# 512 KB weight loads with four pairs of split tiles, and modulation sums in halves, in a hybrid mLSTM and gated-delta encoder block

## The chip, the cores and the metric

The kernel runs on 1 core of a Trainium2 chip. The metric is the device time of one execution in microseconds, the median over runs. TensorE (PE) does the matmuls, with its weight loads shown apart as PEld; VectorE (DVE), ScalarE (ACT) and GpSimd (POOL) do the rest; SyncE (SP) issues most of the DMAs, which 16 DMA engines carry out.

## The reference

One encoder block with batch 1, 256 tokens and width 2048, all in float32. Its weights are some 480 MB and each is used once, so they stream from HBM for the whole run.

```python
c_act = jax.nn.silu(c)
mod = c_act @ ada_w + ada_b                       # 2048 x 12288
shift_m, scale_m, gate_m, shift_f, scale_f, gate_f = jnp.split(mod[:, None, :], 6, axis=-1)
h = rms_norm(x, norm_mix_w) * (1 + scale_m) + shift_m
proj = h @ w_in                                   # split into a_q, a_k, a_v, a_o, a_i, a_f, b_qkv, b_z, b_beta, b_a, merge
h_a = bidirectional(mlstm_chunkwise, ...)         # 4 heads, dk 256, dv 512
y_a = (sigmoid(a_o) * rms_norm(h_a)) @ w_branch_a
o_b = bidirectional(gated_delta_chunkwise, ...)   # 16 heads of 128, chunks of 64, a triangular solve in each
y_b = (rms_norm(o_b) * silu(b_z)) @ w_branch_b
g_a, g_b = jnp.split(jax.nn.sigmoid(merge), 2, axis=-1)
x = x + gate_m * ((g_a * y_a + g_b * y_b) @ w_out)
hf = rms_norm(x, norm_ffn_w) * (1 + scale_f) + shift_f
gt, up = jnp.split(hf @ w_gate_up, 2, axis=-1)
x = x + gate_f * ((silu(gt) * up) @ w_down)       # d_ff 5632
return rms_norm(x, norm_final_w)
```

`mod`, the modulation, is what the change calls by that name: a vector times a 2048 x 12288 matrix, of which two sixths are needed at once and four sixths later.

## The kernel before

**Precision in three products.** A float32 weight is split on the chip: `wh` is its value rounded to the fp32r type (ACT, a copy), `wl` is the remainder (DVE, a subtraction). The activations are split in the same way into a high and a low part, such as `hh`, `hl` for the input projection and `mgh`, `mgl` for `o`. Each product is three matmuls: high by `wh`, low by `wh`, high by `wl`.

**Jobs.** Nearly all weights pass through two generators. `fjob` (L146) makes one column group of the projection with features on the partitions: one load of 1 MB into a `raw` tile (L151, issued by SP), and two halves of it, each split by ACT (L155) and DVE (L156) and followed by 24 matmuls of 128 x 256 (L159 to L161); its jobs are called `b` and `a`. `tjob` (L167) makes 512 columns with tokens on the partitions: a job has several chunks of 1 MB (L177), and each chunk two halves (`halves`, L174), split at L180 and L181, with 12 matmuls of 128 x 512 for each half (L199 to L201). Its jobs are the mLSTM's values and gates (`v`, and an `o` of its own), the GDN gate `z`, the merge gates `mb` and `ma`, the branch projections `yb` and `ya`, the output projection `o` in four column groups of four chunks, and the FFN's `gt`, `up` and `d`. In names such as `wl_o0_1_2` the numbers are job, chunk and half (0 or 2, the first of two row blocks).

**Tiles.** The pool `st` gives `raw` three slots of 1 MB (8 KB on each partition), and `wh` and `wl` three slots each of 512 KB. A load is issued once the tile that had the slot before has been read by its last reader.

**Modulation in the background.** Of the six parts of `mod`, the first two are made with the first projection. Parts 2 to 5 come from `ada_part` (L118): sixteen blocks of 1 MB for each part, loaded into the same `raw` slots (L123) and reduced by one DVE instruction with an accumulator (L124); a last addition brings in the bias. `sums` (L133) makes one block; `pump` (L141) is called once for each chunk of weights and makes a block every `every[0]` calls: every second chunk in GDN groups 1 to 3 and in the branch projections, every fourth in the FFN. In `o`, a list of step numbers says after which halves a block is made (L1130), and whatever is left of part 4 is made at step 4 of the last column group (L1133), because the norm behind `o` needs it.

**Stages.** First the normed input, the first sixteen blocks of the input projection in plain float32, with `loads(b)` (L457) bringing two modulation tiles `ra` and 1 MB of `win0` into a `raw` slot for each of sixteen row blocks; its matmuls are at L507. Then a long mixed stage: four GDN groups and four mLSTM heads are computed by DVE, ACT, POOL and small matmuls, between which the remaining jobs of the input projection are woven. In each GDN group `gdn_invert` solves the triangular systems on DVE (tiles `uu`), which pass through DRAM (`inst_d`, `inv_d`) on the way in and out; `gdn_blocks` (L650) reads the result back as `cg` and transposes it (L652). Then the branch projections `yb` and `ya`, with the merged activations `mg`; then `o`, at whose start `row` (L1064) spreads the gate `gm` over the partitions (products `dg`, a matmul, a copy), and whose column groups each end in `residual` (L1081); then the FFN norm, the FFN, the down projection and the last norm.

**Order.** Within an engine, instructions stand in the order that the tile framework's scheduler gives them; those wrapped in `order(...)` keep their place in the program.

## Time and profile before

| what | value |
|---|---|
| median of 3 runs (lowest to highest) | 2059.3 us (2053.61 to 2061.77) |
| profiled execution: time, span | 2056.24 us, 2054.3 us |
| busy share PE, PEld, DVE, ACT, POOL | 96%, 83%, 68%, 51%, 5% |
| mean granted PE clock | 0.986 |
| bytes moved, mean rate | 485.64 MB, 236 GB/s |
| first projection | to about 138 us, DMA share 1.00 until 130 |
| mixed stage | 138 to 1016 us |
| branch projections | 1016 to 1225 us |
| `o` | 1225 to 1329 us |
| FFN norm | 1329 to 1365 us |
| FFN, down projection, end | 1365 to 2054 us |

The span is the time from the first to the last instruction in the profile. "Busy" counts the time in which an engine has an instruction at work. The DMA share is that of the 16 DMA engines. In rows of waits, "A <- B" is an idle stretch of A that ended when B was done, with the total in us, the count and the mean. The four parts of the modulation that are made in the background take 64 blocks: 23 in the mixed stage, 12 in the branch projections, 13 in `o`, 16 in the FFN.

### The profile page before, as it was taken

The numbers are of one execution on the slowest core, as the hardware profiler recorded it, in microseconds if no ns is written. First come the engines' busy times: TensorE is split into PE (matmuls) and PEld (weight loads), VectorE is DVE, ScalarE is ACT, GpSimd is POOL, SyncE is SP. The second block draws the span as 40 slices with busy tenths as digits, with TensorE's granted clock in tenths as the row PEclk, the third lists the DMA queues.
The fourth block names the chain that finished last, engine by engine and source line by source line (L and its number), as shares of the span: only waits on it lengthen the run. The fifth ranks groups of instructions, "written<-read, shape, count | busy, mean of one in ns | idle before, by whom it ended". The sixth has DMA issues, their size and how long they took to land.

```text
span 2054.3 us, 27035 instructions
## 1 busy us (share of the span) xinstructions
PE 1968.2 (96%) x10374; PEld 1707.0 (83%) x10374; DVE 1394.8 (68%) x2059; ACT 1054.0 (51%) x1584; POOL 106.1 (5%) x205
## 2 busy tenths in 40 slices
PE   8999989999998899999999999889999999999998
PEld 6777779988987898899878787678888888888886
DVE  5787777786888588765667778766656665555554
ACT  3147547856774677466443443364444444444443
POOL 0002210010101010100200000000000000000000
PEclk9999999999999999999999999999999999999999
DMA  9986664566765565666987578756766766555654
GB/s 400 420 321 211 173 216 146 173 190 221 240 224 178 194 207 211 232 247 241 361 295 263 211 264 315 271 184 240 255 243 245 254 238 221 192 204 204 205 203 143
DMA packets 78962, 485.64 MB, mean 236 GB/s; under 512 B 10585, under 2 KB 15969, under 8 KB 24433
## 3 DMA queue, kind: packets, MB, share of 16 engines
q1 hardware_dynamic: 63360, 450.95, 60.9%
q0 software_dynamic: 8160, 17.88, 4.0%
q10 hardware_dynamic: 7314, 15.10, 1.9%
q8 instruction: 81, 1.33, 0.3%
q14 instruction: 47, 0.39, 0.0%
HBM read 467.07 MB, written 16.82 MB: 236 GB/s over the span
## 4 chain that ended last, share of the span: by engine, by line
PE 67%; DVE 13%; DMA 11%; ACT 5%; issue 3%; POOL 1%; ACTq 0%; SPq 0%; DVEq 0%; POOLq 0%
PE acc_up L201 4%; PE acc_up L199 4%; PE acc_up L200 4%; PE acc_d L200 4%; PE acc_d L201 4%; PE acc_d L199 4%; PE acc_gt L200 3%; PE acc_gt L201 3%; PE acc_gt L199 3%; DMA ra<-ada 3%; PE acc_b L161 2%; PE acc_b L159 2%; PE acc_b L160 2%; DMA ada<-ada 2%; PE acc_yb L201 1%
## 5 line engine op out<-in xcount | busy, mean ns | idle before, releaser
L181 DVE TENSOR_TENSOR wl_d<-raw_d,wh_d 128x1024 fp32r<-128x1024 f32 x88 | 107.8, 1225 | 109.1 <-ACT wh_d L180 109.1
L181 DVE TENSOR_TENSOR wl_up<-raw_up,wh_up 128x1024 fp32r<-128x1024 f32 x88 | 107.7, 1225 | 100.4 <-ACT wh_up L180 100.4
L159 PE MATMUL acc_b<-hh,wh_b 128*128 128x256 f32 x576 | 164.1, 285 | 5.8 <-ACT wh_b L155 5.8
L181 DVE TENSOR_TENSOR wl_gt<-raw_gt,wh_gt 128x1024 fp32r<-128x1024 f32 x88 | 107.8, 1225 | 83.2 <-ACT wh_gt L180 83.2
L161 PE MATMUL acc_b<-hh,wl_b 128*128 128x256 f32 x576 | 161.7, 281 | 2.0 <-DVE wl_b L156 2.0
L124 DVE SCALAR_TENSOR_TENSOR ada<-ada,crow 128x2048 f32<-128x2048 f32 x64 | 146.4, 2287 | 25.0 <-DMA ada<-ada 24.8
L160 PE MATMUL acc_b<-hl,wh_b 128*128 128x256 f32 x576 | 160.4, 279 | 0.0
L180 ACT ACTIVATE wh_d<-raw_d 128x1024 fp32r<-128x1024 f32 x88 | 92.9, 1056 | 127.9 <-PE acc_d L200 119.2
L180 ACT ACTIVATE wh_gt<-raw_gt 128x1024 fp32r<-128x1024 f32 x88 | 92.9, 1056 | 118.6 <-PE acc_gt L200 71.0
L180 ACT ACTIVATE wh_up<-raw_up 128x1024 fp32r<-128x1024 f32 x88 | 92.9, 1055 | 108.9 <-PE acc_up L200 78.2
L199 PE MATMUL acc_gt<-wh_gt,hfh 128*128 128x512 f32 x352 | 135.4, 385 | 0.0
L200 PE MATMUL acc_gt<-wh_gt,hfl 128*128 128x512 f32 x352 | 134.7, 383 | 0.1
L201 PE MATMUL acc_gt<-wl_gt,hfh 128*128 128x512 f32 x352 | 133.7, 380 | 0.0
L199 PE MATMUL acc_up<-wh_up,hfh 128*128 128x512 f32 x352 | 133.5, 379 | 0.0
L201 PE MATMUL acc_up<-wl_up,hfh 128*128 128x512 f32 x352 | 133.5, 379 | 0.0
L200 PE MATMUL acc_up<-wh_up,hfl 128*128 128x512 f32 x352 | 133.5, 379 | 0.0
L200 PE MATMUL acc_d<-wh_d,ffl 128*128 128x512 f32 x344 | 131.0, 381 | 0.0
L199 PE MATMUL acc_d<-wh_d,ffh 128*128 128x512 f32 x344 | 131.0, 381 | 0.0
L201 PE MATMUL acc_d<-wl_d,ffh 128*128 128x512 f32 x344 | 130.5, 379 | 0.0
L507 PE MATMUL first<-x,raw 128*128 128x256 f32 x512 | 114.5, 382 | 7.4 <-ACT x L500 6.8
L159 PEld LDWEIGHTS acc_b<-hh,wh_b 128*128 128x128 f32 x576 | 112.5, 195 | 6.4 <-ACT wh_b L155 6.3
L507 PEld LDWEIGHTS first<-x,raw 128*128 128x128 f32 x512 | 96.1, 190 | 25.8 <-ACT x L500 12.4
(369 smaller groups left out, 5275.9 us busy)
## 6 DMA issues: line engine op xcount, KB each, us to landing
ada<-ada SPq DMA_DIRECT2D x64, 1024.0 KB, 5.0
raw_gt<-wgu SPq DMA_DIRECT2D x44, 1024.0 KB, 5.0
raw_up<-wgu SPq DMA_DIRECT2D x44, 1024.0 KB, 4.9
raw_d<-wd SPq DMA_DIRECT2D x44, 1024.0 KB, 4.9
raw_b<-winb SPq DMA_DIRECT2D x36, 1024.0 KB, 5.4
ra<-ada SPq DMA_DIRECT2D x32, 1025.0 KB, 15.7
raw<-win SPq DMA_DIRECT2D x16, 1024.0 KB, 14.5
raw_z<-wint SPq DMA_DIRECT2D x16, 1024.0 KB, 5.8
```

Source lines behind the costliest of these rows:

```text
L124: V.scalar_tensor_tensor(raw, raw, 1.0, row_c[:, :D], ALU.mult, ALU.mult, accum_out=mod[:, c0 + b : c0 + b + 1])
L159: PE.matmul(o, wh[:, k], both(hh, kk).rearrange("p a b -> p b a"), start=kk == 0, stop=False)
L160: PE.matmul(o, wh[:, k], both(hl, kk).rearrange("p a b -> p b a"), start=False, stop=False)
L161: PE.matmul(o, wl[:, k], both(hh, kk).rearrange("p a b -> p b a"), start=False, stop=kk == KB - 1)
L180: order(S.activation(wh, raws[u][:, k0 : k0 + 2], AF.Copy), early)
L181: order(V.tensor_tensor(wl, raws[u][:, k0 : k0 + 2], wh.bitcast(F32), ALU.subtract), early)
L199: order(PE.matmul(ps[t], tok(xh, kk, t), turns(wh[:, k]), start=kk == 0, stop=False), early and steps > 1)
L200: PE.matmul(ps[t], tok(xl, kk, t), turns(wh[:, k]), start=False, stop=False)
L201: PE.matmul(ps[t], tok(xh, kk, t), turns(wl[:, k]), start=False, stop=kk == last)
L507: PE.matmul(first[o], raw[:, o], x[:, b], start=b == 0 and o % 2 == 0, stop=b == KB - 1 and o % 2 == 1)
```

## The change

Every load of weights in `fjob` and `tjob` becomes two of 512 KB, each into a `raw` tile of its own; `raw` has four slots of 512 KB (`NR`) where it had three of 1 MB, and `wh` and `wl` have four slots each (`NW`) where they had three. A modulation block is loaded and reduced in two halves of 512 KB, whose sums land in a tile `mh` and are added at the end of a part; `pump` and `sums` count halves, so that weights and modulation keep their ratio. While `o` runs, the modulation's tiles come from the pool `wp`, six of 512 KB under a tag `ada`, and not from `raw`; before and after they come from `raw`. In the first projection the 1 MB of `win0` comes as two loads, the first into a `raw` slot, the second into a `wl` slot. In `o` every step makes a half block, from step 2 of the first column group on, and the remainder is drained at the same place as before. Number and order of the matmuls in a job stay.

```diff
+NR = 4
+NW = 4
...
-    c1 = st.tile([1, D], F32, tag="raw", bufs=3, name="c1")
-    S.dma_start(c1, crow.unsqueeze(0))
+    c1 = [st.tile([1, D // 2], F32, tag="raw", bufs=NR, name=f"c1_{i}") for i in range(2)]
+    for i in range(2):
+        S.dma_start(c1[i], crow.unsqueeze(0)[:, i * D // 2 : (i + 1) * D // 2])
...
+    ada_in = [st, "raw", NR]
+
     def ada_part(part, row_c):
         c0 = part * KB
+        mh = cp.tile([P, 2, KB], F32, tag="mh", bufs=1, name=f"mh{part}")
         for b in range(KB):
-            raw = st.tile([P, D], F32, tag="raw", bufs=3, name=f"ada{part}_{b}")
-            nc.sync.dma_start(raw, ada4[part - 2, b])
-            V.scalar_tensor_tensor(raw, raw, 1.0, row_c[:, :D], ALU.mult, ALU.mult, accum_out=mod[:, c0 + b : c0 + b + 1])
-            yield True
-        V.tensor_tensor(mod[:, c0 : c0 + KB], mod[:, c0 : c0 + KB], pk[:, PK_ADAB + c0 : PK_ADAB + c0 + KB], ALU.add)
+            for i in range(2):
+                c = slice(i * D // 2, (i + 1) * D // 2)
+                raw = ada_in[0].tile([P, D // 2], F32, tag=ada_in[1], bufs=ada_in[2], name=f"ada{part}_{b}_{i}")
+                nc.sync.dma_start(raw, ada4[part - 2, b][:, c])
+                V.scalar_tensor_tensor(raw, raw, 1.0, row_c[:, c], ALU.mult, ALU.mult, accum_out=mh[:, i, b : b + 1])
+                yield True
+        V.tensor_tensor(mh[:, 0], mh[:, 0], pk[:, PK_ADAB + c0 : PK_ADAB + c0 + KB], ALU.add)
+        V.tensor_tensor(mod[:, c0 : c0 + KB], mh[:, 0], mh[:, 1], ALU.add)
         yield True
...
-        raw = st.tile([P, KB, P], F32, tag="raw", bufs=3, name=f"raw_{name}")
-        nc.sync.dma_start(raw, src)
         for k0 in range(0, KB, 8):
-            wh = st.tile([P, 8, P], F32R, tag="wh", bufs=3, name=f"wh_{name}_{k0}")
-            wl = st.tile([P, 8, P], F32R, tag="wl", bufs=3, name=f"wl_{name}_{k0}")
-            S.activation(wh, raw[:, k0 : k0 + 8], AF.Copy)
-            V.tensor_tensor(wl, raw[:, k0 : k0 + 8], wh.bitcast(F32), ALU.subtract)
+            raw = st.tile([P, 8, P], F32, tag="raw", bufs=NR, name=f"raw_{name}_{k0}")
+            nc.sync.dma_start(raw, src[:, k0 : k0 + 8])
+            wh = st.tile([P, 8, P], F32R, tag="wh", bufs=NW, name=f"wh_{name}_{k0}")
+            wl = st.tile([P, 8, P], F32R, tag="wl", bufs=NW, name=f"wl_{name}_{k0}")
+            S.activation(wh, raw, AF.Copy)
+            V.tensor_tensor(wl, raw, wh.bitcast(F32), ALU.subtract)
             for k in range(8):
                 kk = k0 + k
                 PE.matmul(o, wh[:, k], both(hh, kk).rearrange("p a b -> p b a"), start=kk == 0, stop=False)
                 PE.matmul(o, wh[:, k], both(hl, kk).rearrange("p a b -> p b a"), start=False, stop=False)
                 PE.matmul(o, wl[:, k], both(hh, kk).rearrange("p a b -> p b a"), start=False, stop=kk == KB - 1)
+            pump()
             if k0:
-                pump()
                 done(o.rearrange("p (b a) -> p a b", a=2))
             yield True
...
-        raws = {}
-
         def halves(u, k0):
-            if u not in raws:
-                raws[u] = st.tile([P, 4, 512], F32, tag="raw", bufs=3, name=f"raw_{name}_{u}")
-                nc.sync.dma_start(raws[u], chunks[u])
-            wh = st.tile([P, 2, 512], F32R, tag="wh", bufs=3, name=f"wh_{name}_{u}_{k0}")
-            wl = st.tile([P, 2, 512], F32R, tag="wl", bufs=3, name=f"wl_{name}_{u}_{k0}")
-            order(S.activation(wh, raws[u][:, k0 : k0 + 2], AF.Copy), early)
-            order(V.tensor_tensor(wl, raws[u][:, k0 : k0 + 2], wh.bitcast(F32), ALU.subtract), early)
+            raw = st.tile([P, 2, 512], F32, tag="raw", bufs=NR, name=f"raw_{name}_{u}_{k0}")
+            nc.sync.dma_start(raw, chunks[u][:, k0 : k0 + 2])
+            wh = st.tile([P, 2, 512], F32R, tag="wh", bufs=NW, name=f"wh_{name}_{u}_{k0}")
+            wl = st.tile([P, 2, 512], F32R, tag="wl", bufs=NW, name=f"wl_{name}_{u}_{k0}")
+            order(S.activation(wh, raw, AF.Copy), early)
+            order(V.tensor_tensor(wl, raw, wh.bitcast(F32), ALU.subtract), early)
             return wh, wl
         todo = [(u, k0) for u in range(len(chunks)) for k0 in (0, 2)]
...
-            if k0:
-                pump()
-                if u == len(chunks) - 1:
-                    done(ps)
+            pump()
+            if k0 and u == len(chunks) - 1:
+                done(ps)
             yield True
...
             ra = [w0.tile([P, D + 2], F32, tag="ra", bufs=5, name=f"ra{b}_{i}") for i in range(2)]
-            raw = st.tile([P, N0, P], F32, tag="raw", bufs=3, name=f"raw0_{b}")
+            raw = [
+                st.tile([P, N0 // 2, P], F32, tag=("raw", "wl")[i], bufs=(NR, NW)[i], name=f"raw0_{b}_{i}") for i in range(2)
+            ]
             for i in range(2):
                 order(nc.sync.dma_start(ra[i], ada2[b, :, i]))
-            order(nc.sync.dma_start(raw, win0[b]))
+            for i in range(2):
+                order(nc.sync.dma_start(raw[i], win0[b][:, i * N0 // 2 : (i + 1) * N0 // 2]))
...
     xp = pool(ctx, "xp", side="right")
     wp = pool(sw, "wp")
+    ada_in[:] = [wp, "ada", 6]
     x1 = xp.tile([P, 2, D], F32, name="x1")
...
         for i, _ in enumerate(tjob(f"o{g}", [wo[g, u] for u in range(4)], mgh, mgl, done_o, by_token=between)):
-            if i in ((4, 6, 7), (1, 2, 4, 6), (1, 2, 4, 6), (1, 2, 4))[g]:
+            if i in ((2, 3, 4, 5, 6, 7), range(8), range(8), range(5))[g]:
                 sums()
...
     background.append(ada_part(5, row_c))
+    ada_in[:] = [st, "raw", NR]
     sw.close()
```

At the start of `o`, DVE has the first splits of its weights, the last gating of the branch outputs (`gta`, with the accumulators `acc_ya`), their merge `mg`, the products `dg` for `gm`, and then reductions (`ada`) between splits. Before:

```order
L181 TENSOR_TENSOR wl_o0_0_2_10859<-raw_o0_0_10840,wh_o0_0_2_10858 128x1024
L1000 TENSOR_TENSOR gta3_10632<-gta3_10632,acc_ya3_0_10634 128x512
L1000 TENSOR_TENSOR gta3_10632<-gta3_10632,acc_ya3_1_10635 128x512
L1001 TENSOR_TENSOR mg_9287<-mg_9287,gta3_10632 128x512 x2
L181 TENSOR_TENSOR wl_o0_1_0_10877<-raw_o0_1_10874,wh_o0_1_0_10876 128x1024
L1070 TENSOR_SCALAR dg2_0_10803<-cst_75,mod_85 128x128 x4
L1070 TENSOR_SCALAR dg2_1_10811<-cst_75,mod_85 128x128 x4
L124 SCALAR_TENSOR_TENSOR ada4_3_10926,mod_85<-ada4_3_10926,crow_73 128x2048
```

And after:

```order
L187 TENSOR_TENSOR wl_o0_0_2_11330<-raw_o0_0_2_11327,wh_o0_0_2_11329 128x1024
L187 TENSOR_TENSOR wl_o0_1_0_11348<-raw_o0_1_0_11345,wh_o0_1_0_11347 128x1024
L1008 TENSOR_TENSOR gta3_11093<-gta3_11093,acc_ya3_0_11095 128x512
L1008 TENSOR_TENSOR gta3_11093<-gta3_11093,acc_ya3_1_11096 128x512
L1009 TENSOR_TENSOR mg_9648<-mg_9648,gta3_11093 128x512 x2
L187 TENSOR_TENSOR wl_o0_1_2_11369<-raw_o0_1_2_11366,wh_o0_1_2_11368 128x1024
L1079 TENSOR_SCALAR dg2_0_11272<-cst_75,mod_87 128x128 x4
L1079 TENSOR_SCALAR dg2_1_11280<-cst_75,mod_87 128x128 x4
L1079 TENSOR_SCALAR dg2_2_11288<-cst_75,mod_87 128x128 x4
L132 SCALAR_TENSOR_TENSOR ada4_3_1_11363,mh4_10815<-ada4_3_1_11363,crow_73 128x1024
```

The third split moved ahead of the gating, the fourth stands behind `mg` where the third stood, and the reduction is of half a block. Behind these rows 13 whole reductions alternated with the splits, the last of them in column group 3; now it is 25 half reductions, the last of them between the splits of halves 0 and 2 of chunk 1 of that group.

On SP, the loads of `o` (`raw_o`) and of the modulation (`ada`), in the same place. Before:

```order
L177 DMA raw_o0_2_10908<-wo 128x2048
L123 DMA ada4_3_10926<-ada4 128x2048
L177 DMA raw_o0_3_10945<-wo 128x2048
L123 DMA ada4_4_10963<-ada4 128x2048
L123 DMA ada4_5_10990<-ada4 128x2048
L177 DMA raw_o1_0_10995<-wo 128x2048
```

And after:

```order
L183 DMA raw_o0_3_0_11429<-wo 128x1024
L131 DMA ada4_3_1_11363<-ada4 128x1024
L131 DMA ada4_4_0_11384<-ada4 128x1024
L131 DMA ada4_4_1_11405<-ada4 128x1024
L131 DMA ada4_5_0_11426<-ada4 128x1024
L131 DMA ada4_5_1_11447<-ada4 128x1024
L183 DMA raw_o0_3_2_11450<-wo 128x1024
L131 DMA ada4_6_0_11476<-ada4 128x1024
L183 DMA raw_o1_0_0_11481<-wo 128x1024
```

Modulation loads of several blocks now go out in a row, ahead of weight loads, since they have slots of their own to go to.

In the mixed stage, at the end of the first group's inversion, DVE has the splits of an mLSTM job (`wl_o0` is here the first head's output gate) ahead of the transpose of `cg`, which waits for DRAM. Before:

```order
L181 TENSOR_TENSOR wl_o0_0_0_2042<-raw_o0_0_2039,wh_o0_0_0_2041 128x1024
L181 TENSOR_TENSOR wl_o0_0_2_2058<-raw_o0_0_2039,wh_o0_0_2_2057 128x1024
L181 TENSOR_TENSOR wl_o0_1_0_2076<-raw_o0_1_2073,wh_o0_1_0_2075 128x1024
L181 TENSOR_TENSOR wl_o0_1_2_2092<-raw_o0_1_2073,wh_o0_1_2_2091 128x1024
L652 STREAM_TRANSPOSE cg0_1960<-cg0_1960 128x512
```

And after:

```order
L187 TENSOR_TENSOR wl_o0_0_0_2124<-raw_o0_0_0_2121,wh_o0_0_0_2123 128x1024
L187 TENSOR_TENSOR wl_o0_0_2_2142<-raw_o0_0_2_2139,wh_o0_0_2_2141 128x1024
L187 TENSOR_TENSOR wl_o0_1_0_2160<-raw_o0_1_0_2157,wh_o0_1_0_2159 128x1024
L187 TENSOR_TENSOR wl_o0_1_2_2178<-raw_o0_1_2_2175,wh_o0_1_2_2177 128x1024
L660 STREAM_TRANSPOSE cg0_2038<-cg0_2038 128x512
```

The same splits stand there; only their `raw` tiles are now one for each half.

4 lines of the change are left out of this document (2 added, 2 removed).

## The prediction

> **What bounds the kernel now.** I read the stage table first (columns: length, busy time of PE, PEld, DVE, ACT and POOL, the granted PE clock, the DMA share, GB/s).
>
> ```profile
> 0.00:130.00 130.00, 120.18 (x519) 98.11 (x520) 88.11 (x101) 25.09 (x48) 2.41 (x12) 1.00 1.00 412
> 138.00:1016.00 878.00, 832.59 (x5186) 744.17 (x5185) 656.39 (x1254) 561.25 (x979) 101.59 (x189) 0.98 0.64 215
> 1016.00:1225.00 209.00, 206.10 (x939) 170.12 (x939) 147.75 (x182) 92.53 (x122) 2.13 (x4) 0.98 0.72 257
> 1225.00:1329.00 104.00, 95.15 (x404) 75.94 (x402) 82.02 (x99) 39.71 (x53) 0.00 (x0) 0.97 0.85 313
> 1329.00:1365.00 36.00, 27.30 (x127) 22.16 (x128) 23.82 (x40) 25.55 (x46) 0.00 (x0) 0.95 0.33 116
> 1365.00:2054.00 689.00, 679.15 (x3171) 590.08 (x3169) 390.88 (x377) 303.38 (x326) 0.00 (x0) 1.00 0.62 220
> ```
>
> Stages with different limits. Until 130 us the 16 DMA engines are full (share 1.00). From 1365 us on, FFN and down projection, PE has nothing to gain. In between lie the mixed stage, the branch projections, o (1225 to 1329) and the norm behind it, which the change leaves alone. The profiled execution took 2056.2 us, 3.1 below the median of 2059.3; I sum against it and add the 3.1 at the end.
>
> Next come the waits of PE over the whole span, and the same question asked of the o stage alone.
>
> ```profile
> PE acc_o L201 <- DVE wl_o L181: 8.3, 5, 3.3
> PE first L507 <- ACT x L500: 6.8, 14, 2.1
> PE acc_b L159 <- ACT wh_b L155: 5.8, 3, 2.8
> PE acc_v L201 <- DVE wl_v L181: 5.1, 5, 2.4
> PE px L768 <- ACT obt L770: 4.4, 2, 4.0
> PE acc_z L201 <- DVE wl_z L181: 4.4, 6, 1.2
> ...
> PE pxa L976 <- DVE hal L981: 2.6, 1, 2.6
> ...
> ACT wh_o L180 <- DMA raw_o<-wo: 31.5, 8, 6.1
> DVE wl_o L181 <- ACT wh_o L180: 14.1, 12, 2.5
> ```
>
> In o, ACT waits 31.5 us for weight loads, DVE 14.1 us for ACT. The chain of waits (start, length, what) names the loads that hold PE up. Of `ada`, `raw_b` and `raw_o` it holds ten pieces, of which the first and last of each stage stand here: five in the mixed stage, 30.9 us together, and five in o, 31.4 us, with one more between them that term 3 uses:
>
> ```profile
> 547.10 6.89 DMA ada<-ada
> ...
> 772.50 5.38 DMA raw_b<-winb
> ...
> 1073.41 7.30 DMA ada<-ada
> ...
> 1236.56 6.63 DMA ada<-ada
> ...
> 1292.62 6.97 DMA ada<-ada
> ```
>
> So where modulation loads and weight loads share the three `raw` slots, the latency of a 1 MB load sets the pace.
>
> **The price of a 512 KB load** is not in the trace as such. Its bounds are other transfers (median us to landing):
>
> ```profile
> ada<-ada SPq DMA_DIRECT2D x64, 1024.0 KB, 5.0
> ...
> gtb<-mb_d SPq DMA_DIRECT2D x4, 512.0 KB, 7.4
> ...
> gta<-ma_d SPq DMA_DIRECT2D x4, 512.0 KB, 5.3
> ...
> outT<-x SPq DMA_DIRECT2D x8, 256.0 KB, 2.4
> ```
>
> Low end 2.4 (half the size), high end 7.4 (a load of that size queued behind others). I take 2.4 + (5.0 - 2.4) / 3 = 3.3 us, on the line between the undisturbed transfers of the same queue, so 1.7 less than now.
>
> **Term 1, the o stage.** Its matmuls run from 1225.6 to 1328.4 (times of one, lowest, median, highest in ns, then first start and last end). One half is 12 matmuls; ACT, held only by PE, starts one every 2.59 us:
>
> ```profile
> L199 PE MATMUL acc_o<-wh_o,mgh x120: 379/379/780, 1225.6 to 1322.7; 128*128 128x512 f32 x120
> ...
> L220 PE MATMUL acc_o<-wl_o,mgh x8: 379/379/380, 1323.8 to 1328.4; 128*128 128x512 f32 x8
> ...
> 1196.01 1.06 ACT L180 ACTIVATE wh_ya<-raw_ya 128x1024 fp32r<-128x1024 f32 x1 [1.53 <-PE acc_ya L200]
> 1198.60 1.06 ACT L180 ACTIVATE wh_ya<-raw_ya 128x1024 fp32r<-128x1024 f32 x1 [1.53 <-PE acc_ya L200]
> ...
> 1227.59 1.22 DVE L181 TENSOR_TENSOR wl_o<-raw_o,wh_o 128x1024 fp32r<-128x1024 f32 x1
> ...
> 1258.00 2.36 DVE L181 TENSOR_TENSOR wl_o<-raw_o,wh_o 128x1024 fp32r<-128x1024 f32 x2
> ...
> L124 DVE SCALAR_TENSOR_TENSOR ada<-ada,crow x13: 2283/2292/2294, 1230.3 to 1312.2; 128x2048 f32<-128x2048 f32 x13
> L124 DVE DVE_READ_ACCUMULATOR ada<-ada,crow x13: 80/83/85, 1232.6 to 1314.4; 128x1 f32 x13
> ...
> L497 DVE SCALAR_TENSOR_TENSOR x<-x,m,rows x16: 480/485/486, 17.4 to 127.8; 128x256 f32<-128x256 f32 x16
> ```
>
> PE needs 32 x 2.59 = 82.9 us, plus about 4 for the rows of `gm` and the last transposes: it could end near 1225.6 + 87 = 1312.6 instead of 1328.4. With a pool of six for the modulation weights, the four `raw` slots serve o alone: a weight load goes out when the split four halves before it is done, 10.4 us ahead, and 3.3 us land in time. What is late next is DVE. A half reduction costs, from the rows at 256 and 2048 elements, 0.485 + 768 x (2.292 - 0.485) / 1792 = 1.26 us plus 0.083 to read the accumulator; two cost 2.69 where one cost 2.37, so each 1 MB dearer by 0.31. (Bounds: half of 2.37, no increase, and a second full 2.29.) In the listing the fourth split follows `mg` where the third stood, so it ends at 1228.8. From there to the split of half 28, the first behind all reductions, DVE has 24 splits at 1.18 (28.3), 25 half reductions at 1.34 (33.5), 16 `dg` (under 4), two `mgl` (1.2), three residuals at 2.4 (7.2) and small sums (0.5): 74 us, up to 1303. Five halves of PE work, 13 us, follow: the end is at 1316, a gain of 13. DVE waits for ACT now and then, 14.1 us of it in the old stage, so I take **-10** (between -16, PE alone, and -4).
>
> **Term 2, the mixed stage.** The five loads of its chain shrink by 5 x 1.7 = 8.5 us at most; PE's waits that hang on them are the 5.8 for `wh_b` and small ones for `wl_b`. I take -5 (0 to -8). The fourth pair gives a wait behind a busy DVE 2.59 us more, but not everywhere: in the listing at `cg0` no split moved ahead, and there PE waits longest.
>
> ```profile
> 305.74 0.71 DVE L652 STREAM_TRANSPOSE cg<-cg 128x512 f32<-128x512 f32 x1 [7.26 <-DMA cg<-inv_d]
> ...
> 307.88 0.48 PE L201 MATMUL acc_o<-wl_o,hh 128*128 128x512 f32 x1 [3.33 <-DVE wl_o L181]
> ```
>
> Time won before such a place is waited away there: the inversion's round trip through DRAM is unchanged. The waits of this kind are `acc_v` and `acc_z` above and smaller ones, some 20 us; I take -4 (0 to -10). Against it, 23 reductions run here, 23 x 0.31 = 7 us more DVE, which is off the path in part: +3. Sum **-6** (-15 to +7).
>
> **Term 3, branch projections.** The 2.6 us at `pxa` stand in the chain behind a 7.3 us modulation load; 12 reductions cost 3.7 us more DVE, mostly idle there. **-2** (-4 to +2).
>
> **Term 4, the first stage.** Queue q1 pays 316 ns a packet of 7.1 KB, queue q10 85 ns for 2.1 KB (share x 2054.3 x 16 / packets), 22.5 and 24.3 GB/s an engine, so smaller pieces move no slower.
>
> ```profile
> q1 hardware_dynamic: 63360, 450.95, 60.9%
> ...
> q10 hardware_dynamic: 7314, 15.10, 1.9%
> ...
> raw<-win SPq DMA_DIRECT2D x16, 1024.0 KB, 14.5
> ```
>
> `win0`'s 16.8 MB at 24.3 instead of 412 / 16 = 25.8 would take 2.6 us longer; a gain is excluded by the share of 1.00. **+1**. The rule "Batch DMAs to ≥1 MiB" (the Trainium skill, DMA: Bandwidth & Descriptors, Measured) speaks against the change, and its fit, 2.0 us plus bytes / 436e3, puts a 512 KB load at an estimated 3.2 us. The 14.5 us to landing beside full engines shows loads queued, with the fixed part hidden. By the rule unhidden, 16 added loads would be +32 us instead of +1.
>
> **Term 5, the clock.** Beside the worst waits for `acc_b` the granted clock of a 50 us stretch was 0.90, which is another 5 us.
>
> ```profile
> 700.00:750.00 50.00, 46.74 (x329) 44.26 (x330) 37.58 (x69) 34.85 (x67) 3.56 (x7) 0.90 0.60 197
> ...
> 699.99 0.38 PE L159 MATMUL acc_b<-hh,wh_b 128*128 128x256 f32 x1 [2.82 <-ACT wh_b L155]
> ```
>
> With the waits shorter I take **-2** (0 to -5). The clock drops to half after an idle window of some 3.4 us (the Trainium skill, TensorE: Matmul & The Clock Gate, Part 1); the rows show shorter waits beside a lowered clock, so by that rule alone the term would be 0.
>
> **Costed at nothing.** FFN: a load and its split turn a slot over in 3.3 + 1.06 + 1.23 = 5.6 us, four slots give one per 1.4 us, and PE asks for five loads (one of them modulation) per four halves, one per 2.07 us; the cover is gone only above 6.0 us to landing. Its 16 dearer reductions (5 us) lie on a DVE busy 391 of 689 us. The doubled issues on SP, 0.33 us each, wait behind nothing but slots. The extra `tensor_tensor` per part is 0.2 us, four times.
>
> Sum: -10 - 6 - 2 + 1 - 2 = -19; 2056.2 - 19 + 3.1 = 2040.
>
> **Rivals.** (a) The gain in o is real, but the rest gives nothing: earlier PE work waits at the DRAM round trips, and 48 dearer reductions before o's end (48 x 0.31 = 15 us of DVE) eat the remainder. Then o's 10 less some 3: 2059.3 - 7 = 2052. For it: `cg0`; against it: PE's waits for `acc_b` follow loads. (b) The split waits before 1365 us go nearly all, some 33 us by the rows above and the smaller ones, with them term 3's 2.6 and term 5's 5: 2059.3 - 40 = 2019. Against it: the same round trips. (c) Slower: in the mixed stage and the projections every third load is modulation, so four slots must turn over three loads per 5.18 us. Now three slots have 10.4 us for 5.0 to 5.4 of landing plus about 4.9 of splitting; then four have 6.9 us, less 2.3 of splitting: it turns at 4.6 us to landing. At `gta`'s 5.3 a load comes every 1.90 instead of 1.73 us, times some 210 loads +36: 2059.3 - 10 + 36 = 2085. For it `gta` and `gtb`, against it the 2.4 of `outT`. (d) In the first stage the 16 added loads each pay an unhidden fixed part, by rows 2.4 - 0.9 = 1.5 us: +24, so 2064; the full engines speak against it. The rule of the Trainium skill above (DMA: Bandwidth & Descriptors, Measured) would be this case with its own 2.0 us a load; no row here shows it.
>
> **How the numbers follow.** Forecast 0.52 (2030 to 2049), (a) 0.22 (2049 to 2059), (b) 0.16 (2010 to 2030), (c) 0.06, (d) 0.04. A measurement of this kernel tells about 0.5% (10 us) from no change. Faster by more: the forecast, (b) and a little of (a), 0.70; within: 0.20; slower: 0.10. The range 2022 to 2057 leaves out (c), (d), half of (b) and the top of (a).
>
> **What would show it.** No DMA piece of `raw_o` in the chain, o some 94 us long with DVE over 85 us busy; 512 KB loads landing in 3 to 4 us; waits for `wh_b` below 2 us; the 3.3 us at `cg0` still there; half reductions at 1.26 us; the stage after 1365 unchanged at 689; the first at full DMA share, 131 us. Wrong if loads land above 4.6 us, if DVE becomes the longest piece of the chain in the mixed stage, or if PE waits appear in FFN.

## The result: slower, and the profile after

The changed kernel takes 2135.8 us (median of 4 runs, 2133.6 to 2137.8) against 2060.1 before: a ratio of 1.039, interval 1.037 to 1.041, so about 76 us slower, where 2040 was forecast. Its profiled execution takes 2133.6 us; its span of 2131.6 is 77.3 longer than that of before. The stages, by the matmuls of each (times of one in ns, then the first and the last start, which the prediction calls an end):

```profile
L515 PE MATMUL first<-x,raw x512: 378/379/484, 18.5 to 138.8; 128*128 128x256 f32 x171
L205 PE MATMUL acc_yb<-wh_yb,obh x128: 379/379/781, 1045.0 to 1170.7; 128*128 128x512 f32 x128
L205 PE MATMUL acc_o<-wh_o,mgh x120: 379/379/1414, 1281.2 to 1372.0; 128*128 128x512 f32 x120
L225 PE MATMUL acc_o<-wl_o,mgh x8: 379/379/380, 1373.1 to 1377.7; 128*128 128x512 f32 x8
L205 PE MATMUL acc_d<-wh_d,ffh x344: 379/379/780, 1888.9 to 2115.8; 128*128 128x512 f32 x172
```

And before (the rows of `o` stand in the prediction):

```profile
L507 PE MATMUL first<-x,raw x512: 378/379/483, 18.5 to 137.9; 128*128 128x256 f32 x171
L199 PE MATMUL acc_yb<-wh_yb,obh x128: 379/379/780, 1016.9 to 1126.0; 128*128 128x512 f32 x128
L199 PE MATMUL acc_d<-wh_d,ffh x344: 378/379/780, 1811.3 to 2038.2; 128*128 128x512 f32 x172
```

The mixed stage is counted from the last `first` to the first `acc_yb`, the projections from there to the first `acc_o`, `o` to its own last matmul, norm and FFN from there to the first `acc_d`. By these rows, the first stage ends 0.9 us later, the mixed stage takes 906.2 us instead of 879.0, the branch projections 236.2 instead of 208.7, `o` 96.5 instead of 102.8, norm and FFN up to the first matmul of `d` 511.2 instead of 482.9, and the row of `d` 226.9 in both. So 27, 28 and 28 us were lost in three stages of quite different work, and 6 won in `o`. What the three have in common is that modulation loads share the `raw` slots there. `d`, which has no modulation, did not change.

The table by stage (columns as in the prediction) shows PE short of work in all three, at a lower granted clock:

```profile
139.00:1045.00 906.00, 844.11 (x5189) 758.66 (x5188) 654.58 (x1296) 560.62 (x979) 102.14 (x189) 0.96 0.66 207
1045.00:1281.00 236.00, 214.52 (x937) 174.52 (x937) 155.01 (x216) 95.18 (x125) 2.13 (x4) 0.95 0.71 235
1281.00:1378.00 97.00, 90.43 (x402) 75.53 (x400) 79.34 (x120) 39.38 (x52) 0.00 (x0) 0.96 0.89 326
1383.00:1889.00 506.00, 480.55 (x2217) 415.70 (x2217) 288.04 (x308) 223.53 (x250) 0.00 (x0) 0.98 0.68 217
```

Over the span PE is idle 139.9 us instead of 86.1 and busy 1991.7 instead of 1968.2 with the same 10374 matmuls: 54 us are waits; the other 23 are longer matmuls, at a mean granted clock of 0.970 instead of 0.986.

The waits name what came last. The third number of such a row is the longest wait, here and in the rows ahead of the prediction and in it, and not the mean as it is called there; no sum used it. One row is DVE's, the others PE's; before, DVE waited 24.8 us in 18 waits for modulation, and PE not at all at `pxf`, the transposes of the gated FFN activations.

```profile
DVE ada L132 <- DMA ada<-ada: 190.3, 84, 7.2
...
PE pxf L1225 <- DVE sg L1219: 20.5, 8, 4.0
PE pb L751 <- DVE r L752: 10.6, 6, 2.8
...
PE pxa L984 <- DVE hal L989: 7.4, 1, 7.4
```

PE waits less than before for split weights (all rows of `wh_` and `wl_` together 39 us before, 26 now; `wh_b`, 5.8 before, is gone from the list) and more for everything else (36 before, 104 now). Most of that is DVE's other work, and DVE waits for modulation loads. A place in the FFN shows how. First the loads' queue, then DVE, last PE (start, length, and in brackets the idle time ahead and what ended it):

```profile
1478.45 0.33 SPq L131 DMA_DIRECT2D ada<-ada  x1
...
1477.20 1.23 DVE L187 TENSOR_TENSOR wl_gt<-raw_gt,wh_gt 128x1024 fp32r<-128x1024 f32 x1 [0.94 <-ACT wh_gt L186]
1479.79 1.23 DVE L187 TENSOR_TENSOR wl_gt<-raw_gt,wh_gt 128x1024 fp32r<-128x1024 f32 x1 [1.37 <-ACT wh_gt L186]
1483.40 1.23 DVE L132 SCALAR_TENSOR_TENSOR ada<-ada,crow 128x1024 f32<-128x1024 f32 x1 [2.38 <-DMA ada<-ada]
...
1485.68 1.28 DVE L1219 TENSOR_TENSOR sg<-sg,acc_up 128x512 f32<-128x512 f32 x2
...
1486.42 0.44 PE L1225 MATMUL pxf<-cst,sg 128*128 128x128 f32 x2 [1.93 <-DVE sg L1219]
```

The split that ends at 1478.43 frees a slot; the modulation load goes out at 1478.45; DVE has one more split to do and stands before the reduction at 1481.02, 2.6 us after the issue. The load lands 4.9 us after it, so DVE stands still for 2.4 us. The gating `sg` stands behind it and one more split, and PE's transposes wait 1.9 us for `sg`. The same place before the change:

```profile
1434.61 0.33 SPq L123 DMA_DIRECT2D ada<-ada  x1
...
1438.54 1.23 DVE L181 TENSOR_TENSOR wl_gt<-raw_gt,wh_gt 128x1024 fp32r<-128x1024 f32 x1 [1.36 <-ACT wh_gt L180]
1439.68 2.28 DVE L124 SCALAR_TENSOR_TENSOR ada<-ada,crow 128x2048 f32<-128x2048 f32 x1
```

There two splits stand between, the load went out 5.1 us ahead, and the reduction starts with no wait. I call this distance the lead: from the issue of a modulation load to the moment when DVE is ready for its reduction. And the landing became only a little shorter with the load (median us from issue to landing, by size):

```profile
ada<-ada SPq DMA_DIRECT2D x128, 512.0 KB, 5.0
raw_gt<-wgu SPq DMA_DIRECT2D x88, 512.0 KB, 4.6
raw_up<-wgu SPq DMA_DIRECT2D x88, 512.0 KB, 4.5
raw_d<-wd SPq DMA_DIRECT2D x88, 512.0 KB, 4.5
raw_b<-winb SPq DMA_DIRECT2D x72, 512.0 KB, 4.9
```

The same five had 4.9 to 5.4 at 1 MB. The 5.0 of `ada` mixes `o`, where several of its loads go out in a row and land after 8.2 us (median), with the other stages: there a half lands after 4.5 to 4.9 us, a whole block after 4.8 to 6.0. So a half load needs nearly the lead of a whole one, some 4.5 to 5 us, and the listing (the order in which the scheduler puts the instructions) gives it about half.

### The profile page after: what moved, and what is told of

Read it like the earlier page. It is cut to its first block, busy times and chain, and to the rows that moved or that the text cites. A ratio compares the mean times of both kernels' runs of the same rounds, so it can differ in the third digit from the quotient of the medians.

```text
span 2131.6 us, 27989 instructions
## 1 busy us (share of the span) xinstructions
PE 1991.7 (93%) x10374; PEld 1731.1 (81%) x10374; DVE 1399.4 (66%) x2191; ACT 1056.3 (50%) x1586; POOL 106.7 (5%) x205
## 4 chain that ended last, share of the span: by engine, by line
PE 51%; DMA 23%; DVE 15%; ACT 5%; issue 5%; POOL 1%; DVEq 0%; ACTq 0%; POOLq 0%; SPq 0%
DMA ada<-ada 11%; DMA ra<-ada 6%; PE acc_d L207 3%; PE acc_d L205 3%; PE acc_d L206 3%; PE acc_gt L207 3%; PE acc_gt L206 3%; PE acc_gt L205 3%; PE acc_up L206 3%; PE acc_up L205 3%; PE acc_up L207 3%; PE acc_o L207 2%; PE acc_o L205 2%; PE acc_o L206 2%; PE acc_b L168 1%
## 5 line engine op out<-in xcount | busy, mean ns | idle before, releaser
L132 DVE SCALAR_TENSOR_TENSOR ada<-ada,crow 128x1024 f32<-128x1024 f32 x128 | 156.6, 1224 | 190.5 <-DMA ada<-ada 190.3
L515 PEld LDWEIGHTS first<-x,raw 128*128 128x128 f32 x512 | 96.1, 190 | 27.0 <-ACT x L508 14.6
```

Source lines behind the costliest of these rows:

```text
L132: V.scalar_tensor_tensor(raw, raw, 1.0, row_c[:, c], ALU.mult, ALU.mult, accum_out=mh[:, i, b : b + 1])
L515: PE.matmul(first[o], raw[o // (N0 // 2)][:, o % (N0 // 2)], x[:, b], start=b == 0 and o % 2 == 0, stop=b == KB - 1 and o % 2 == 1)
```

## The experiments

Three theories. **A, order:** the listing puts a half reduction too few splits behind its load, and DVE, which works in order, stands still with everything queued behind. **B, slots:** modulation and weights get in each other's way in four shared slots of 2 MB, where before there were 3 MB. **C, pieces:** smaller DMA pieces and dearer sums cost the time by themselves. The main numbers first; the lead is the median in us of parts 2, 3 and 5 of `mod` (part 2 is made in the mixed stage, 3 there and in the projections, 5 in the FFN), the wait is DVE's for modulation over the span, and the stages are by the rows of PE's matmuls, in us. Leads are left blank where the pieces moved to other stages or were not counted. Each ratio below is to the kernel before in the same session, where its median was 2055.7 to 2056.8 us.

| kernel | median us | lead 2, 3, 5 | wait | mixed | projections | o | norm, FFN |
|---|---|---|---|---|---|---|---|
| before | 2060 | 6.9, 5.0, 5.1 | 24.8 | 879.0 | 208.7 | 102.8 | 482.9 |
| changed | 2136 | 4.3, 2.8, 2.6 | 190.3 | 906.2 | 236.2 | 96.5 | 511.2 |
| held | 2165 | 4.3, 2.6, 4.8 | 144.2 | 904.1 | 237.1 | 96.2 | 522.0 |
| ring6 | 2116 | 4.1, 3.4, 2.6 | 202.9 | 919.6 | 217.0 | 94.4 | 501.9 |
| ring6held | 2161 | | | 930.1 | 216.7 | 94.0 | 519.7 |
| twodma | 2073 | | 67.7 | 887.9 | 218.0 | 109.3 | 484.2 |
| ownring | 2108 | | 67.7 | 919.5 | 207.7 | 97.2 | 500.6 |
| adawhole | 2105 | | 46.6 | 934.4 | 207.7 | 98.7 | 484.2 |
| poolonly | 2050 | 6.3, 5.0, 5.1 | 29.1 | 876.0 | 210.2 | 96.1 | 483.7 |
| nopool | 2153 | 4.3, 2.5, 2.6 | 198.5 | 907.1 | 236.0 | 114.6 | 511.0 |
| held2 | 2103 | 4.2, 2.7, 7.7 | 123.4 | 903.5 | 233.9 | 96.0 | 485.9 |
| heldall | 2061 | 7.6, 6.9, 7.7 | 15.6 | 880.4 | 217.3 | 95.3 | 485.3 |
| heldall6 | 2034 | 13.1, 11.9, 10.2 | 6.1 | 863.0 | 206.2 | 96.8 | 483.6 |
| nw3 | 2123 | 4.3, 3.0, 2.6 | 192.6 | 910.6 | 219.5 | 97.0 | 514.0 |
| beforeheld | 2046 | 10.5, 10.9, 10.2 | 3.9 | 866.2 | 203.5 | 103.3 | 483.7 |
| poolheld | 2032 | 10.5, 11.5, 10.2 | 1.4 | 867.5 | 204.5 | 90.4 | 484.1 |

**held.** The order is kept in the FFN for reductions and splits.

```diff
-                V.scalar_tensor_tensor(raw, raw, 1.0, row_c[:, c], ...)
+                order(V.scalar_tensor_tensor(raw, raw, 1.0, row_c[:, c], ...), every[0] == 4)
...
-            order(V.tensor_tensor(wl, raw, wh.bitcast(F32), ALU.subtract), early)
+            order(V.tensor_tensor(wl, raw, wh.bitcast(F32), ALU.subtract), early or every[0] == 4)
```

> The changed kernel, but in the FFN the DVE reductions and weight splits keep the order of the program, so that a half reduction stands behind three splits after the one that frees its slot, and not behind one. Loads, slots, pairs and sums are as in the change. Theory (lead): a modulation load can go out only when its slot is free, 2.59 us a split ahead of the reduction that needs it, and lands after about 5 us; DVE waits out the difference and PE waits for what is queued behind. With three splits, 7.8 us, the load is there: DVE's waits for modulation in the FFN go, from gt's first matmul to d's the FFN takes some 478 us instead of 506, and the time is 2108 (2100 to 2116), the 28 us that the FFN lost. The earlier stages stay as slow. Rival (pieces): smaller DMA pieces and dearer sums themselves cost the time; then 2136, within 5.

2165.0, ratio 1.054 (1.051 to 1.058): slower still. DVE's waits for modulation in the FFN fell from 67.5 to 12.8 us (of a window from 1390 to 1800), but the FFN and `d` grew. The splits were held too, and so the splits of the next gate stood behind `sg` and `ffl`, which wait for PE:

```profile
PE acc_gt L207 <- DVE wl_gt L187: 26.0, 10, 2.6
...
PE acc_d L207 <- DVE wl_d L187: 11.2, 3, 3.8
```

The time is outside both forecasts. The edit moved two things; it tells nothing on the theories, except that the places of the splits count as much.

**ring6.** Six slots, three pairs.

```diff
-NR = 4
-NW = 4
+NR = 6
+NW = 3
```

> The changed kernel with six raw slots of 512 KB (3 MB, as before the change) and three pairs of split tiles instead of four of each. In the listing of DVE the scheduler now puts a modulation reduction mostly 3 to 5 splits behind the one that frees its slot in the mixed stage and the branch projections, but directly behind it (0 splits) in the FFN. Lead theory: the mixed stage and the projections recover, o begins near 1230 us instead of 1281; the FFN gets worse, DVE waits some 4.5 us for each of 30 reductions there, and the FFN takes 510 to 550 us; in all 2110 (2085 to 2140). Rival (pieces): nothing recovers, o begins at 1275 to 1285, FFN 506, 2136. Second rival (depth: 3 MB of slots is all that counts): 2045, FFN 478.

2115.8, ratio 1.030 (1.027 to 1.033). The time lies in A's range, but by luck: the FFN's 502 is short of what A expected, and the mixed stage did not recover as I had read from the listing; it got worse. My count of splits went by the order in which slots come up, and the trace shows other leads: 4.1, 3.4 and 2.6 us, hardly longer than with four slots, and DVE waits 202.9 us. More slots alone do not bring the leads back, so B in its simple form (depth alone brings 2045) is out; the projections recovered 19 us while DVE's waits for modulation there stayed (40.2 us, 45.3 in the change). For that I have no shown cause.

**ring6held** put both together.

> The kernel with six raw slots and three pairs, and the program's order kept in the FFN (a reduction then stands 4 splits behind the one that frees its slot). Lead theory: nothing waits for modulation, the mixed stage as before or a little shorter, o 6 to 10 us shorter than before by its pool, FFN as before: 2048 (2035 to 2060). Rival (pieces): 2130 or more.

2160.6, ratio 1.052 (1.048 to 1.055). In the FFN and in `d` it repeats held: the same 26.0 and 11.2 us of waits for splits. The miss is that of the held splits.

**twodma.** Before, each 1 MB load as two DMAs into one tile.

```diff
-            nc.sync.dma_start(raw, ada4[part - 2, b])
+            for h_ in (0, D // 2):
+                nc.sync.dma_start(raw[:, h_ : h_ + D // 2], ada4[part - 2, b][:, h_ : h_ + D // 2])
```

(And so in `fjob` and `tjob`.)

> The kernel before, with every 1 MB load of weights and modulation issued as two DMAs of 512 KB into the two halves of the same 1 MB tile; slots, splits, reductions and their order stay as before. Lead theory: 2060 within 10, since no slot is freed earlier or later; the number of packets rises as in the changed kernel. Rival (pieces): slower, 2090 to 2136, since the packets are those of the changed kernel.

2073.0, ratio 1.010 (1.006 to 1.013), between the two theories. With the packets of the changed kernel (117072 on the loads' queue, 63360 before) it loses 17 us and not 76, 1 of it in the FFN; DVE waits 67.7 us for modulation instead of 24.8. A lead that was just enough is short when a block's second part is issued later; that is an argument, not shown apart from the packets here. Nor did the order stay as the expectation says: in the trace some splits and other work stand at other places on DVE and ACT than before. So the 17 us have no shown cause; what halves cost once the order is held, poolheld tells below.

**ownring** and **adawhole** give the modulation slots of its own all the time, with three pairs: two slots for halves (the edit shown), or one for whole blocks, loaded and reduced as before the change.

```diff
-NW = 4
+NW = 3
...
-    ada_in = [st, "raw", NR]
+    ada_in = [st, "ada", 2]
```

> The changed kernel with three pairs of split tiles instead of four, and the modulation halves in two slots of their own all the time (the weights keep four slots). So far: from the issue of a modulation load to the moment DVE is ready for its reduction the trace of before has 5.1 to 6.9 us (medians by part), that of the changed kernel 2.6 to 4.3 outside o, with six raw slots 2.6 to 4.1 too, while the load lands after 5.0 in all. Theory A (order): the listing puts a reduction of a half behind fewer splits than its load needs, whatever the slots; here 15 of the 32 in the FFN still stand at most one split behind: 2085 (2065 to 2110). Theory B (slots): modulation and weights get into each other's way in the shared slots; with slots of their own DVE's waits for modulation fall from 190 to below 30 us and the time is 2045 (2035 to 2060).

> The changed kernel with three pairs instead of four, and the modulation in whole blocks of 1 MB again, loaded and reduced as before the change, in one slot of 1 MB of its own (in o three of them in the pool of its own); the weights stay in halves. Beside the kernel with two own slots of half the size, which takes the same space, it differs in the size of the modulation pieces alone. Theory A (order): the listing puts 2 to 4 splits, 5 to 10 us, between the instruction that frees the slot and most reductions; DVE waits less than 40 us for modulation, and the time is 2055 (2040 to 2070). Theory B (slots): the same as with two own slots of half the size, within 10. Rival (pieces): 2090 or more, as the weights still come in halves.

2108.4, ratio 1.025 (1.022 to 1.028), and 2105.0, ratio 1.023 (1.019 to 1.026). Neither is a clean test. Freed from the weights' ring, the listing drew the modulation forward by hundreds of us into the mixed stage, where DVE is busy for some 72% of the time: the first reduction starts at 139.5 and 145.1 us, against 490.4 in the changed kernel, and the last of adawhole is done before the FFN begins.

```profile
L132 DVE SCALAR_TENSOR_TENSOR ada<-ada,crow x128: 1187/1218/1227, 139.5 to 1466.0; 128x1024 f32<-128x1024 f32 x128
```

```profile
L129 DVE SCALAR_TENSOR_TENSOR ada<-ada,crow x64: 2259/2284/2293, 145.1 to 1363.7; 128x2048 f32<-128x2048 f32 x64
```

The mixed stage paid 40 and 55 us over before. B's 2045 did not come: slots of its own don't bring the time back, though with the reductions elsewhere that is no clean refutation. ownring's 2108 lies in A's range, by luck for the same reason. A's 2055 for adawhole failed, since I had not looked at where the reductions would go; its time lies where B (within 10 of ownring) and C (2090 or more) had put it, and with the reductions moved it speaks for neither.

**poolonly** is the kernel before with the pool for `o` alone (three whole blocks); **nopool** is the change without its pool.

```diff
     wp = pool(sw, "wp")
+    ada_in[:] = [wp, "ada", 3]
```

> The kernel before, with one part of the change: while o runs, the modulation blocks (whole, 1 MB) come from a pool of their own, three tiles, and not from raw. Everything else as before. If the shared slots held up o as the prediction says, o takes 94 to 97 us instead of 102.8 and the time is 2052 (2046 to 2057). Rival: DVE, 82 us busy there, is late next and o stays at 100 or more: 2058 (2055 to 2063).

> The changed kernel without its pool for o: modulation halves come from the four raw slots there too. If the pool is what made o 96.5 us long, o grows to 105 to 115 and the time to 2148 (2142 to 2156), since DVE waits for modulation loads in o as it does in the stages ahead. Rival: the halves made it, and o stays below 99, the time at 2136.

2050.0, ratio 0.997 (0.995 to 0.999), with `o` at 96.1 us; and 2152.8, ratio 1.047 (1.044 to 1.050), with `o` at 114.6. Both times lie where the forecasts for the pool had them. In nopool's `o` ACT waits for weight loads as it did before the change, and more:

```profile
ACT wh_o L186 <- DMA raw_o<-wo: 47.4, 19, 5.5
```

So all of `o`'s gain is the pool's: with whole loads it gives 6.7 us, and the rest of the change without it costs 12 there.

**held2.** In the FFN the reductions alone are held: the first half of held's diff, without the second. Each of them moves two splits back in the listing, at the place shown above behind `sg` and `ffl`.

> The changed kernel, but in the FFN the half reductions alone keep the place that the program gives them; the weight splits and all else are free as in the change. In the listing each of 32 reductions moves two splits back on DVE (three splits, not one, stand between the split that frees its slot and the reduction), the orders of SP and ACT are the same row for row, and PE has 16 pairs of rows exchanged. (The kernel that held the splits too had put the gating and the low parts of the FFN's activations ahead of four splits, and PE waited 26 us there.) Theory A (order): DVE's 67 us of waits for modulation in the FFN fall below 10, the FFN from the end of o to d's first matmul is 484 (482 to 488) instead of 511, the earlier stages stay, and the time is 2109 (2104 to 2113). Theory B or C (shared slots, or the pieces themselves): 2136, within 4, since slots, loads and pieces are unchanged.

2102.9, ratio 1.022 (1.020 to 1.024). This is the clean one: loads, slots, sums and the orders of SP and ACT are those of the change, row for row in the traces; 32 reductions stand two splits later on DVE, and on PE 16 pairs of rows are exchanged. The FFN is back at 485.9 us (25 of the 28 lost), DVE waits for no modulation there, and the lead is 7.7 us. The place from above:

```profile
1468.91 0.33 SPq L131 DMA_DIRECT2D ada<-ada  x1
...
1473.98 1.28 DVE L1219 TENSOR_TENSOR sg<-sg,acc_up 128x512 f32<-128x512 f32 x2
1475.43 1.23 DVE L187 TENSOR_TENSOR wl_gt<-raw_gt,wh_gt 128x1024 fp32r<-128x1024 f32 x1 [0.17 <-ACT wh_gt L186]
1476.58 1.29 DVE L245 TENSOR_TENSOR ffl<-pxf,ffh 128x512 fp32r<-128x512 f32 x2
1477.78 1.22 DVE L132 SCALAR_TENSOR_TENSOR ada<-ada,crow 128x1024 f32<-128x1024 f32 x1
```

The gating goes ahead of the reduction, and the load has had 8.9 us. The time is 1 us under A's range, since the stages ahead, in the same order, came out some 5 us shorter too. B and C, which expected no change, are refuted for the FFN.

**heldall** holds the reductions in all stages (the edit shown), **heldall6** has six slots and three pairs besides.

```diff
-                V.scalar_tensor_tensor(raw, raw, 1.0, row_c[:, c], ...)
+                order(V.scalar_tensor_tensor(raw, raw, 1.0, row_c[:, c], ...))
```

> The changed kernel with every half reduction in its place in the program, in all stages. In the listing two splits or more then stand between the split that frees a slot and the reduction in the mixed stage and the branch projections, where the change has none or one, and three in the FFN. Theory A (order): two splits are 5.2 us against 5.0 us of landing; DVE's waits for modulation fall from 190 to 40 us or less, the mixed stage to 890 (880 to 900), the projections to 215 (208 to 222), the FFN to 484: 2077 (2060 to 2095). Theory B or C: 2130 or more.

> The same with six raw slots and three pairs of split tiles; four splits then stand ahead of a reduction (10.4 us). Theory A (order): nothing waits for modulation outside the end of o; the mixed stage at 885 (875 to 895), the projections 208 to 212, o 94 to 98, the FFN 484: 2063 (2045 to 2075). With six slots alone, without the order, it was 2116. Rival (the mixed stage loses by the places of the weight splits, which the listing also moved): the mixed stage stays above 900 and the time above 2080.

2061.4, ratio 1.002 (1.001 to 1.003), and 2033.9, ratio 0.989 (0.987 to 0.991): the first at the fast end of A's range, the second faster than it. One word of order takes back 74 us; DVE's waits for modulation fall from 190.3 to 15.6 us, the mixed stage goes from 906 to 880, the projections from 236 to 217. It is less clean than held2: ahead of the FFN, splits and other work on DVE and some of ACT's moved with the reductions, so for these stages it shows the order's worth and not that of the reductions' places alone. With longer leads (six slots) the mixed stage is 16 us shorter than before, and PE's busy time in the projections is full:

```profile
139.00:1002.00 863.00, 825.58 (x5191) 738.21 (x5190) 657.09 (x1299) 561.31 (x979) 101.78 (x189) 0.99 0.69 216
1002.00:1208.00 206.00, 205.73 (x937) 169.92 (x936) 151.57 (x213) 94.20 (x124) 2.13 (x4) 0.98 0.78 269
1208.00:1305.00 97.00, 89.85 (x402) 74.92 (x400) 80.23 (x121) 40.41 (x52) 0.00 (x0) 0.96 0.90 331
1310.00:1788.00 478.00, 473.22 (x2218) 409.53 (x2217) 287.92 (x307) 222.47 (x249) 0.00 (x0) 0.99 0.71 228
```

Slots lengthen the leads once the order lets them: with four and six slots the leads of part 2 are 7.6 and 13.1 us here, 4.3 and 4.1 without the order. The 27 us between heldall and heldall6 can be the slots' or the pairs', as four pairs became three; no run with the order held parts them.

**nw3.** The change with three pairs.

> The changed kernel with three pairs of split tiles instead of four, all else as in the change. It tells what the fourth pair does. If the loss is in the order of the modulation's reductions, which here stand as in the change (none or one split behind), the time is 2136, within 10. If the fourth pair moved splits ahead of other work on DVE in the mixed stage and that cost the time there, the mixed stage is back at 885 or less and the time at 2115 or less.

2122.9 (2112 to 2129), ratio 1.031 (1.028 to 1.035), between the two forecasts: DVE's wait stays at 192.6 us. The mixed stage and the FFN are no better; 17 us come back in the projections, though DVE still waits 40.1 us for modulation there. So the fourth pair gives nothing here and costs some 13 us. In the projections PE's longest wait in the change, 7.4 us at `pxa`, is 2.0 here; why is open.

**beforeheld** and **poolheld.** The order alone, and order and pool, on the kernel before with its whole loads.

```diff
-            V.scalar_tensor_tensor(raw, raw, 1.0, row_c[:, :D], ...)
+            order(V.scalar_tensor_tensor(raw, raw, 1.0, row_c[:, :D], ...))
```

> The kernel before, with its whole 1 MB reductions held in their place in the program, no halves and no pool. In the listing three to four splits then stand between the one that frees a slot and a reduction outside o, where before had one to six. If the halves themselves bring part of the 22 us that the kernel with held halves and six slots gained on before, this one stays within 10 us of before in the mixed stage and the projections: 2050 (2045 to 2058). If only the order of the reductions mattered, it gains in the mixed stage what that kernel did (863 instead of 879): 2038 (2030 to 2044), o unchanged at 103.

> The same with the pool of three 1 MB tiles for o. It differs from the kernel with held halves, six slots and the pool (2034) in the size of the loads and sums alone; slots and pairs take the same space. If size does nothing once the order is held: 2034, within 6. If halves give something: 2042 (2038 to 2050), with the difference in the mixed stage, where loads of 1 MB hold a slot longer.

2045.8, ratio 0.995 (0.993 to 0.997), and 2031.8, ratio 0.990 (0.987 to 0.994). By its time beforeheld lies in the range for halves, by its stages in the other: the mixed stage is 866 us, 13 shorter than before, with the order alone, and `o` is unchanged. poolheld and heldall6, whose loads and sums differ in size and take the same space, lie 2 us apart, within their intervals: with the order held, halves neither gain nor lose in sum (4.5 us less in the mixed stage, 6.4 more in `o`). So with the order held C's smaller pieces cost nothing that can be told from zero; whether they cost something while it is free, as perhaps in twodma, is open. Both beat before and the change; poolheld, with 1 MB loads and three pairs, is some 20 to 25 us under before and about 100 under the change.

That heldall comes back to the time of before hides a second loss. Held alike, before with the pool takes 2032 and the change 2061: some 29 us remain, and six slots with three pairs take back 27 of them. So slots or pairs cost the change something beside the order; which of the two is open.

## Why the prediction was wrong

**The price of a half load** failed. The prediction took 3.3 us, by a line between the undisturbed 256 KB and 1 MB transfers; measured are 4.5 to 5.0, against 4.9 to 5.4 for whole ones. The row nearest in size and kind was `gta`, 512 KB in 5.3 us; the price left it out, and only rival (c) used it. The text's own mark, wrong if loads land above 4.6 us, was passed by `ada` and `raw_b`. The rule that was weighed there (the Trainium skill, DMA: Bandwidth & Descriptors, Measured) speaks against small loads, and its figures are for DMAs issued from GpSimd, where these go out on SP. The trace agrees that a half load takes far more than half the time of a whole one, and not with the estimate of 3.2 us; and with the order held, the smaller loads cost the kernel nothing (heldall6 2034, poolheld 2032).

**The FFN at nothing** is the step whose failure is shown best: 28 us lost, 25 of them back in held2. The working compared rates: a slot turns over in 5.6 us, four slots give one load per 1.4 us, PE asks for one per 2.07. That a reduction stands one split, 2.59 us, behind the instruction that frees its slot is no rate. It could have been read from the listing, where before showed two splits and the change one; the prediction counted splits there at `cg` and `o`, and did not count them at the sums. The right price would not have saved this step: by its own rule the cover goes above 6.0 us to landing, and the loads of the FFN landed after 4.5 to 4.6. Its mark, PE waits in the FFN, came true at `pxf`.

**Term 2, the mixed stage** (-6, -15 to +7) was +27, and **term 3, the projections** (-2) +28. The sum priced a half reduction as 0.31 us more work for each block. That size was nearly right: 1.224 us and 0.083 to read the accumulator, against 1.26 and 0.083 expected, so 0.24 more for each block. What failed is that the terms had no wait of DVE for modulation in them: over the span 190 us. heldall takes back 26 and 19 of these two losses; in the projections three pairs alone take back 17 as well, so the order is not the whole cause there. At `cg0`, on which the text looked, the splits stood as it said, and PE's wait of 3.3 us is still there.

**Term 1, o** (-10, -16 to -4) was -6.3: the pool's gain, by poolonly and nopool, as the mechanism said; no piece of `raw_o` is in the chain of waits there any more. (The working's end at 1316 is 12.4 us ahead of 1328.4, and not 13.) The one DMA piece of that chain is 11.1 us at the start of `o`, a modulation load again: DVE stands before its reduction for 7.2 us, and PE waits 5.8 for the products `dg` behind it. DVE was busy 79 us and not over 85:

```profile
1283.34 11.14 DMA ada<-ada
```

**Term 4, the first stage** (+1) was +0.9, at a DMA share of 1.00. **Term 5, the clock** (-2) had the sign wrong with the waits: PE's matmuls took 23 us more, at 0.970 instead of 0.986.

**The rivals.** Rival (c) was nearest: slower above 4.6 us to landing, at 2085. The condition was met. Its mechanism, slots that turn over too slowly, is not what the runs showed for these 76 us: six slots without the order keep the leads and the waits, and four slots with it are within 0.3% of before. No rival named the place of the sums, and the range ended at 2057.

**What stays open.** Why the listing places a half's reduction at half the lead of a whole one; how much of the losses of the mixed stage and the projections is the reductions' place alone; the 17 to 19 us that the projections win with three pairs; whether slots or pairs make the 27 us between heldall and heldall6; and the 17 us of twodma, whose packets, later landing and changed order were not told apart.

## What to carry to other kernels

A load is hidden if its issue lies far enough ahead of its reader in the reader's own queue. Count in the listing what stands between the instruction that frees the slot and the one that needs the load, multiply by the rhythm of that stage, and compare with the landing time that the trace shows for that queue; a rate of slots against a rate of requests doesn't tell it. When a change makes pieces smaller, do that again for every reader, above all for background work on an engine whose later instructions are on the path; to hold such work back in the order is cheap, and gave here more (74 us) than sizes, slots and pairs together (27 to 29 with the order held).

## What the runs showed of the hardware

A load of 512 KB on SP's queue landed in 4.5 to 5.0 us where one of 1 MB took 4.9 to 5.4 (medians of the five rows above), although a packet's own time on that queue fell from 316 to 182 ns (share x span x 16 / packets):

```profile
q1 hardware_dynamic: 119376, 450.97, 63.6%
```

And waits of PE went with a lower granted clock: 54 us of added waits, 45 of them in waits of over 2 us (23 of these, 11 before), came with 23 us more for the same matmuls. The other runs lie roughly on the same line, for example: with PE idle for 75 us of the span (poolheld) the mean granted clock is 0.993, with 86 (before) 0.986, 96 (heldall) 0.983, 121 (held2) 0.976, 140 (the change) 0.970, 163 (held) 0.968. That the waits lower the clock is not shown apart from this.
